# Splitting fetch from preparation of token tiles, and adding two directions' outputs from the PSUM bank

## The chip, the cores and the metric

The kernel runs on one core of a Trainium2 chip. The metric is device time of one execution in microseconds; three executions of the kernel before gave 3358.46, 3360.61 and 3367.17 us, so the median is 3360.61 us.

## The reference

One layer of a bidirectional encoder over 2048 tokens of width 1024, in float32. A layer norm gives `h`; one input projection feeds two head groups, and their outputs are concatenated into one output projection; then follow a layer norm, a squared-ReLU MLP and a last layer norm. The parts that matter here:

```python
def hybrid_mixer(h, w_in, ..., w_out):
    proj = h @ w_in
    ...
    y_ssd = ssd_bidir(z, xbc, dt_raw, conv_w, conv_b, dt_bias, a_log, d_skip, ssd_norm_g)
    y_rwkv = rwkv7_bidir(rw, mu_rwkv, w0, w_up, a0, a_up, g_up, k_k, k_a, r_k, lnx_g, lnx_b)
    y = jnp.concatenate([y_ssd, y_rwkv], -1).astype(h.dtype)
    return y @ w_out
...
# the end of ssd_bidir:   y = y * silu(z); y * rsqrt(mean(y*y) + RMS_EPS) * norm_g
# the end of rwkv7_bidir:
    _, ys = lax.scan(rwkv7_step, S0, inputs)
    y = ys[forward] + flip(ys[backward])
    y = ((y - mean) * lax.rsqrt(var + GN_EPS)) * lnx_g + lnx_b   # per head of 64
    return (y + bonus) * g
```

`rwkv7_step` is a recurrence over tokens, run once forward and once backward; the two outputs of a token are added before the group norm.

## The kernel before, in words

The kernel works in three phases. `phase_in` normalises, projects and runs most of the SSD group. `phase_rwkv` (line 936) runs the RWKV recurrence in chunks of 128 tokens, and weaves the output projection into it as filler for TensorE. `phase_mlp` (line 1358) follows.

**The recurrence.** There are 32 steps `u`. Step `u` treats head group `pg = u % 2` and chunk `s = u // 2`, both directions at once: the forward direction treats the tokens of chunk `s`, the backward direction those of chunk `15 - s` (`UN` is 16). Four generators make up the work of a step, and `weave` (line 1260) interleaves their pieces with fixed weights: `chain(u)` (line 1136), the serial part, has 12 pieces; `finish(u - 1)` (line 1207) gets weight 10 and runs from `FL` = 0.4 to `FH` = 1.0 of the chain; `merge`, `inverse` and `prep` prepare later steps.

`chain(u)` collects the outputs of both directions in one PSUM bank, `yp` (line 1154; the pool has one buffer), by the matmuls of lines 1165 and 1192. Line 1182 (`zt`), lines 1185 and 1186 carry the state to the next step of the head group on VectorE. At the end (lines 1194 to 1205) ScalarE copies each direction's outputs out of the bank (line 1202) and a DMA stores them to the scratch tensor `yaD` (line 1203). From `s` = 8 on, each token tile then has both directions' outputs in `yaD`. `finish` loads both (line 1213), adds them on GpSimd (line 1214), centres the sum per head with a matmul (line 1219), squares it on ScalarE (line 1222), sums the squares with a matmul (line 1225), takes the root and the reciprocal (lines 1228, 1230), scales, adds the bonus and multiplies by the gate (lines 1239 to 1249), and stores to `yR` (line 1250).

**The output projection.** `out_pieces` (line 785) is a generator of filler. It visits the 16 token tiles twice in one order: first with the SSD half of the weights, and a second time with the RWKV half, and then the layer norm. `load` (line 813) fetches a token tile from DRAM (residual `h`, outputs `yr`, in the first pass also the broadcast root mean squares `rsb`), scales `yr` on VectorE in the first pass (line 823), and splits it into a high and a low part on ScalarE (line 825) and GpSimd (line 827). `products` (line 830) does 24 matmuls (line 838) in eight pieces of three, and adds the results to `h` on VectorE (lines 841, 843). Most pools of this generator have two buffers a name. The next token is loaded ahead of the products of the present one (line 896).

**What sets the order.** `dense(ins, n)` (line 1074) is called at eight points of a step at most (once after each product of `chain` and of `merge` that has a weight). Each call adds a credit, and takes pieces from the filler until it has met a piece that yields `DENSE`; a piece that yields `HELD` ends the call and leaves at most one credit. `tc.issue_after` ties the filler's TensorE instructions behind the instruction given. In the second pass token `j` is held until step `FA + j` = 19 + `j`; tokens that do not fit are drained in `phase_mlp`, between its first preparations (lines 1434 to 1438). All loads and stores are issued by SyncE (SP), in one queue. The whole program is put in order by `tile.TileContext(nc, schedule_with_timeline_sim=True)` (line 1681): the written order is a priority among the instructions that are ready.

Of the kernel before, what the change touches and what calls it, by code (L numbers as in the profile page):

```python
# [9 lines left out]
F32 = mybir.dt.float32  # L10
F32R = mybir.dt.float32r
AF = mybir.ActivationFunctionType
ALU = mybir.AluOpType
# [3 lines left out]
P = 128  # L17
# [767 lines left out]
def out_pieces(k):  # L785
# [3 lines left out]
    with ExitStack() as ctx:  # L789
# [20 lines left out]
                yield  # L810
            k.wo = wh, wl

        def load(t, ys, first):
            h = wk.tile([P, D], F32, name="h")
            nc.sync.dma_start(h, k.hD[t])
            yr = wk.tile([P, 4, P], F32, name="yr")
            for g in range(2):
                nc.sync.dma_start(yr[:, 2 * g:2 * g + 2], ys[g][:, :, P * t:P * t + P].rearrange("a p t -> p a t"))
            if first:
                rsb = wk.tile([P, 2, P], F32, name="rsb")  # L820
                nc.sync.dma_start(rsb, rsD[:, t].unsqueeze(0).broadcast_to([P, 2, P]))
                for c in range(4):
                    nc.vector.scalar_tensor_tensor(yr[:, c], yr[:, c], ppc(k, "ng", c), rsb[:, c // 2], ALU.mult, ALU.mult)
            yh = wk.tile([P, 4, P], F32R, name="yh")
            nc.scalar.copy(yh, yr)
            yl = wk.tile([P, 4, P], F32R, name="yl")
            nc.gpsimd.tensor_tensor(yl, yr, yh, ALU.subtract)
            return t, h, yh, yl
# [62 lines left out]
        nc.sync.dma_start(rsD.rearrange("g c t -> (g c) t"), rt)  # L891
        yield
        order = [t for s in range(NT // 2, NT) for t in (NT - 1 - s, s)]
        ops = load(order[0], k.yS, True)
        for j in range(NT):
            nxt = load(order[j + 1], k.yS, True) if j + 1 < NT else None
            yield
            yield from products(ops, True)
            ops = nxt
        ws = weights(4)  # L900
        next(ws)
        for p in gates((0, 3)):
# [15 lines left out]
        for j in range(NT):  # L918
            while not ready(j):
                yield HELD  # L920
            if nxt:
                ops = nxt
            else:
                ops = load(order[j], k.yR, False)
                for _ in range(HL):
                    yield HELD
            while k.u < FA + j // FB:
                yield HELD
            nxt = load(order[j + 1], k.yR, False) if ready(j + 1) else None
            yield  # L930
            yield from products(ops, False, rows)
            k.finals = j + 1
            yield LAST


def phase_rwkv(k):
    nc, tc, I = k.nc, k.tc, k.I
    with ExitStack() as ctx:
# [32 lines left out]
        def pairs(ap):  # L971
            return ap.rearrange("a p t -> p a t")
# [163 lines left out]
        def chain(u):  # L1136
# [14 lines left out]
                return out, mm  # L1151


            yp = k.psy.tile([P, 2, 2, 2, 64], F32, name="yp")
            for c in range(2):
                yield
# [37 lines left out]
            ZV.pop(u)  # L1194
            fin = FIN[u] = []
            for d in range(2):
                nat = s if d == 0 else UN - 1 - s
                yv = yp[:, d].rearrange("p r c t -> p r (c t)")
                if d:
                    yv = yv[:, :, ::-1]  # L1200
                ya = sm.tile([P, 2, P], F32, name="ye")
                nc.scalar.copy(ya, yv)
                nc.sync.dma_start(pairs(k.yaD[pg][2 * d:2 * d + 2, :, P * nat:P * nat + P]), ya)
                if s >= UN // 2:
                    fin.append(nat)

        def finish(u):

            pg, fin = u % 2, FIN.pop(u)
            fin = [(nat, sm.tile([P, 2, P], F32, name="ya")) for nat in fin]  # L1210
            for nat, ya in fin:
                yo = sm.tile([P, 4, P], F32, name="yo")
                nc.sync.dma_start(yo, pairs(k.yaD[pg][:, :, P * nat:P * nat + P]))
                nc.gpsimd.tensor_tensor(ya, yo[:, 0:2], yo[:, 2:4], ALU.add)
            yield
            sds = []
            for nat, ya in fin:
                cp_ = k.ps.tile([P, 2, P], F32, name="ps")
                nc.tensor.matmul(cp_, rc[:, R_CEN:R_CEN + P], ya, start=True, stop=True)
                (nc.scalar.copy if CA else nc.vector.tensor_copy)(ya, cp_)  # L1220
                sq = wk.tile([P, 2, P], F32, name="sq")
                nc.scalar.activation(sq, cp_, AF.Square)
                yield
                vp = k.ps.tile([P, 2, P], F32, name="ps")
                nc.tensor.matmul(vp, k.cst[:, C_BLK:C_BLK + P], sq, start=True, stop=True)
                yield
                sd = sm.tile([P, 2, P], F32, name="sd")
                nc.scalar.activation(sd, vp, AF.Sqrt, bias=k.eps[:, 2:3], scale=1.0 / 64)
                for pr in range(2):
                    nc.vector.reciprocal(sd[:, pr], sd[:, pr])  # L1230
                sds.append(sd)
            for (nat, ya), sd in zip(fin, sds):
                tok = slice(P * nat, P * nat + P)
                bon = wk.tile([P, 2, P], F32, name="bon2")
                nc.sync.dma_start(bon, pairs(k.bD[pg][:, :, tok]))
                gate = wk.tile([P, 2, P], F32, name="gate")
                nc.sync.dma_start(gate, pairs(k.gD[pg][:, :, tok]))
                yield
                nc.vector.tensor_tensor(ya, ya, sd, ALU.mult)
                for pr in range(2):  # L1240
                    p = 2 * pg + pr
                    if TA:
                        nc.scalar.activation(ya[:, pr], ya[:, pr], AF.Identity, scale=ppc(k, "lnx_g", p), bias=ppc(k, "lnx_b", p))
                    else:
                        nc.vector.tensor_scalar(ya[:, pr], ya[:, pr], ppc(k, "lnx_g", p), ppc(k, "lnx_b", p), ALU.mult, ALU.add)
                yield
                nc.gpsimd.tensor_tensor(bon, ya, bon, ALU.add)
                o = wk.tile([P, 2, P], F32, name="o")
                (nc.gpsimd if OG else nc.vector).tensor_tensor(o, bon, gate, ALU.mult)
                nc.sync.dma_start(pairs(k.yR[pg][:, :, tok]), o)  # L1250
                k.final[nat] += 1
# [29 lines left out]
        for u in range(-AH, U):  # L1281
            jobs = []
            if 0 <= u - 1 and FIN[u - 1]:
                fin = finish(u - 1)
                if FE:
                    next(fin)
                jobs.append((fin, 10, FL, FH, 0))
            if 0 <= u + MG < U:
                jobs.append((merge(u + MG), 5, ML, 0.9, PM))
            if 0 <= u + AH - 1 < U:  # L1290
                jobs.append((inverse(u + AH - 1), 16, IL, IH, PI))
            if u + AH < U:
                jobs.append((prep(u + AH), 18, 0.0, PH, PP_))
            k.u = u
            jobs.append((k.ssd, SR, 0.0, 1.0, PS))
            weave(chain(u) if u >= 0 else iter([None] * 12), jobs)
# [388 lines left out]
```

## Time and profile before

| | us |
|---|---|
| median of three executions | 3360.61 |
| lowest, highest | 3358.46, 3367.17 |
| the profiled execution | 3365.71 |
| its span from the first to the last instruction | 3363.9 |
| TensorE busy in that span | 2999.4 |
| VectorE busy | 2166.7 |
| ScalarE busy | 1535.1 |
| GpSimd busy | 1584.2 |

All times in the profile come from that one execution and count from its first instruction. PE is TensorE's matmul, PEld its weight load, DVE is VectorE, ACT is ScalarE, POOL is GpSimd, SPq is the queue of SyncE that issues the DMAs; L1202 is line 1202 of the kernel. A group row reads: line, engine, operation, output<-inputs, shapes, count | busy us, mean ns of one | idle us of the engine just before them and what ended it. A row of waits reads: who waited for whom: us in total, times, longest. A row of the timeline reads: start, duration in us, engine, line, operation, tiles, count, and in brackets the idle time before it.

### The profile page before, as it was taken

The numbers are of one execution on the slowest core, as the hardware profiler recorded it, in microseconds if no ns is written. First come the engines' busy times: TensorE is split into PE (matmuls) and PEld (weight loads), VectorE is DVE, ScalarE is ACT, GpSimd is POOL, SyncE is SP. The second block draws the span as 40 slices with busy tenths as digits, with TensorE's granted clock in tenths as the row PEclk, the third lists the DMA queues.
The fourth block names the chain that finished last, engine by engine and source line by source line (L and its number), as shares of the span: only waits on it lengthen the run. The fifth ranks groups of instructions, "written<-read, shape, count | busy, mean of one in ns | idle before, by whom it ended". The sixth has DMA issues, their size and how long they took to land. (4 is left out here: it accounts for less than half of the span.)

```text
span 3363.9 us, 63959 instructions
## 1 busy us (share of the span) xinstructions
PE 2999.4 (89%) x23783; PEld 2394.6 (71%) x23783; DVE 2166.7 (64%) x3671; ACT 1535.1 (46%) x2993; POOL 1584.2 (47%) x1972
## 2 busy tenths in 40 slices
PE   5979999988887799898898886999899989999997
PEld 3767877766675577676666664888787868887886
DVE  7798556667666455554577658767877744466446
ACT  3556323333334445455565544544544553344333
POOL 0352124444445333334466665555566335555645
PEclk9989999889886688897798887999999989999998
DMA  6445355776778666666666554777799475566554
GB/s 209 135 157 185 120 148 176 199 214 195 201 205 251 150 165 161 155 167 163 170 181 174 142 155 152 234 252 234 258 323 314 141 297 190 198 213 212 189 197 153
DMA packets 728183, 650.23 MB, mean 193 GB/s; under 512 B 204064, under 2 KB 578496, under 8 KB 727232
## 3 DMA queue, kind: packets, MB, share of 16 engines
q1 hardware_dynamic: 727872, 646.15, 62.5%
q8 instruction: 187, 3.06, 0.4%
q14 instruction: 124, 1.02, 0.1%
HBM read 403.43 MB, written 242.57 MB: 192 GB/s over the span
## 5 line engine op out<-in xcount | busy, mean ns | idle before, releaser
L1553 DVE TENSOR_TENSOR ul<-ul,uh 128x1024 fp32r<-128x1024 f32 x112 | 241.3, 2156 | 293.9 <-ACT uh L1552 293.6
L1553 POOL TENSOR_TENSOR pl<-pl,ph 128x1024 fp32r<-128x1024 f32 x112 | 287.9, 2575 | 277.9 <-ACT ph L1552 277.8
L1507 PE MATMUL ps<-hh,wh 128*128 128x512 f32 x896 | 352.2, 394 | 19.8 <-ACT wh L1370 6.6
L266 PE MATMUL psg<-hh,wh 128*128 128x512 f32 x864 | 357.2, 414 | 7.3 <-ACT u L285 6.6
L1611 PE MATMUL ps<-ph,uh 128*128 128x512 f32 x896 | 349.0, 392 | 10.4 <-ACT ph L1552 8.7
L1611 PE MATMUL ps<-pl,uh 128*128 128x512 f32 x896 | 351.6, 393 | 5.0 <-POOL pl L1553 5.0
L267 PE MATMUL psg<-hh,wl 128*128 128x512 f32 x864 | 354.5, 410 | 0.0
L268 PE MATMUL psg<-hl,wh 128*128 128x512 f32 x864 | 353.2, 410 | 1.4 <-DVE hl L236 1.4
L1507 PE MATMUL ps<-hl,wh 128*128 128x512 f32 x896 | 350.6, 392 | 1.5 <-DVE hl L1430 1.4
L1507 PE MATMUL ps<-hh,wl 128*128 128x512 f32 x896 | 351.0, 392 | 0.9 <-DVE wl L1371 0.9
L1611 PE MATMUL ps<-ph,ul 128*128 128x512 f32 x896 | 350.4, 392 | 0.0
L1371 DVE TENSOR_TENSOR wl<-wa,wh 128x512 fp32r<-128x512 f32 x217 | 209.5, 970 | 88.9 <-ACT wh L1370 87.9
L1065 POOL TENSOR_TENSOR ltmp<-ln,la 128x30 f32<-128x30 f32 (+10 forms) x480 | 123.6, 258 | 255.7 <-DMA la<-ad 225.6
L1552 ACT CAST ph<-pl 128x1024 fp32r<-128x1024 f32 x112 | 117.7, 1051 | 274.2 <-DMA pl<-pD 274.2
L1370 ACT CAST wh<-wa 128x512 fp32r<-128x512 f32 x217 | 133.0, 618 | 207.2 <-POOL wa L1343 100.2
L1507 PEld LDWEIGHTS ps<-hh,wh 128*128 128x128 f32 x896 | 169.8, 190 | 59.2 <-ACT wh L1370 7.9
L266 PEld LDWEIGHTS psg<-hh,wh 128*128 128x128 f32 x864 | 169.6, 196 | 47.4 <-ACT u L285 8.1
L1611 PEld LDWEIGHTS ps<-ph,uh 128*128 128x128 f32 x896 | 169.4, 189 | 47.0 <-ACT ph L1552 9.5
L1611 PEld LDWEIGHTS ps<-pl,uh 128*128 128x128 f32 x896 | 169.8, 190 | 43.9 <-POOL pl L1553 8.7
L268 PEld LDWEIGHTS psg<-hl,wh 128*128 128x128 f32 x864 | 168.4, 195 | 39.7 <-issue 3.4
L1507 PEld LDWEIGHTS ps<-hl,wh 128*128 128x128 f32 x896 | 169.5, 189 | 37.5 <-DVE hl L1430 1.8
L267 PEld LDWEIGHTS psg<-hh,wl 128*128 128x128 f32 x864 | 169.7, 196 | 36.3 <-issue 2.6
(322 smaller groups left out, 7087.6 us busy)
## 6 DMA issues: line engine op xcount, KB each, us to landing
uD<-ua SPq DMA_DIRECT2D x224, 256.0 KB, 2.9
ul<-uD SPq DMA_DIRECT2D x112, 512.0 KB, 4.6
pl<-pD SPq DMA_DIRECT2D x112, 512.0 KB, 3.7
wa<-in_w_fc_dram SPq DMA_DIRECT2D x124, 256.0 KB, 3.4
pD<-sc SPq DMA_DIRECT2D x112, 256.0 KB, 4.2
rk<-rk SPq DMA_DIRECT2D x64, 384.0 KB, 4.7
h<-hD SPq DMA_DIRECT2D x48, 512.0 KB, 4.0
eD<-et SPq DMA_DIRECT2D x32, 514.0 KB, 2.7
```

The source lines that it names most:

```text
L266: nc.tensor.matmul(pt, wh[:, c], hh[:, c], start=(c == 0), stop=False)
L267: nc.tensor.matmul(pt, wl[:, c], hh[:, c], start=False, stop=False)
L268: k.lag = nc.tensor.matmul(pt, wh[:, c], hl[:, c], start=False, stop=(c == KC - 1))
L1065: eng.tensor_tensor(tv, ln[:, 0:m, r:r + 1].broadcast_to([P, m, w]), la[:, r:r + 1, r + 1:16].broadcast_to([P, m, w]), ALU.mult)
L1370: nc.scalar.copy(hi, x)
L1371: nc.vector.tensor_tensor(lo, x, hi, ALU.subtract)
L1507: nc.tensor.matmul(pt, x, y, start=(n == 0 and i not in (2, 3)), stop=(n == 11 and i not in (1, 5)), skip_group_check=True)
L1552: nc.scalar.copy(hi, x)
L1553: eng.tensor_tensor(lo, x, hi, ALU.subtract)
L1611: nc.tensor.matmul(banks[j], x, z, start=(g == 0 and s == 0), stop=(g == NG - 1 and s == 5))
```

## The change

`load` becomes two functions. `fetch` issues the DMAs only; `prepare` has the VectorE scaling and the split. A helper `after` runs the products of a token and calls `prepare` for the next token when the sixth of the eight pieces comes up. The first token of the first pass is prepared four held calls behind its fetch, and a fifth held call follows; in the second pass a token that is not prefetched is prepared behind its two held calls.

In `chain`, from `s` = 8 on, the other direction's stored outputs are loaded at the start of the step into `yo`, and at its end a VectorE add takes the bank and `yo` and writes the sum to `ya`, which `finish` uses at once. The store of these steps, and `finish`'s load and GpSimd add, are gone. In `finish` a second `yield` stands between the square and its matmul, and its weight is 12 in place of 10.

```diff
-        def load(t, ys, first):
+        def fetch(t, ys, first):
             h = wk.tile([P, D], F32, name="h")
             nc.sync.dma_start(h, k.hD[t])
...
                 nc.sync.dma_start(rsb, rsD[:, t].unsqueeze(0).broadcast_to([P, 2, P]))
+                return t, h, yr, rsb
+            return t, h, yr, None
+
+        def prepare(raw):
+
+            t, h, yr, rsb = raw
+            if rsb is not None:
                 for c in range(4):
                     nc.vector.scalar_tensor_tensor(yr[:, c], yr[:, c], ppc(k, "ng", c), rsb[:, c // 2], ALU.mult, ALU.mult)
             yh = wk.tile([P, 4, P], F32R, name="yh")
...
-        ops = load(order[0], k.yS, True)
+        def after(pieces, raw, n=5):
+
+            ops = None
+            for i, p in enumerate(pieces):
+                if p is DENSE:
+                    if i == n and raw:
+                        ops = prepare(raw)
+                    yield p
+            return ops
+
+        raw = fetch(order[0], k.yS, True)
+        for _ in range(4):
+            yield HELD
+        ops = prepare(raw)
+        yield HELD
         for j in range(NT):
-            nxt = load(order[j + 1], k.yS, True) if j + 1 < NT else None
+            raw = fetch(order[j + 1], k.yS, True) if j + 1 < NT else None
             yield
-            yield from products(ops, True)
-            ops = nxt
+            ops = yield from after(products(ops, True), raw)
...
-                ops = load(order[j], k.yR, False)
+                raw = fetch(order[j], k.yR, False)
                 for _ in range(HL):
                     yield HELD
+                ops = prepare(raw)
...
-            nxt = load(order[j + 1], k.yR, False) if ready(j + 1) else None
+            raw = fetch(order[j + 1], k.yR, False) if ready(j + 1) else None
             yield
-            yield from products(ops, False, rows)
+            nxt = yield from after(products(ops, False, rows), raw)
...
+            nats = [s, UN - 1 - s]
+            others = []
+            for d in range(2) if s >= UN // 2 else ():
+                yo = sm.tile([P, 2, P], F32, name="yo")
+                nc.sync.dma_start(yo, pairs(k.yaD[pg][2 - 2 * d:4 - 2 * d, :, P * nats[d]:P * nats[d] + P]))
+                others.append(yo)
+
             yp = k.psy.tile([P, 2, 2, 2, 64], F32, name="yp")
...
-                ya = sm.tile([P, 2, P], F32, name="ye")
+                ya = sm.tile([P, 2, P], F32, name="ye", bufs=4)
+                if s >= UN // 2:
+                    nc.vector.tensor_tensor(ya, yv, others[d], ALU.add)
+                    fin.append((nat, ya))
+                    continue
                 nc.scalar.copy(ya, yv)
                 nc.sync.dma_start(pairs(k.yaD[pg][2 * d:2 * d + 2, :, P * nat:P * nat + P]), ya)
-                if s >= UN // 2:
-                    fin.append(nat)
...
-            fin = [(nat, sm.tile([P, 2, P], F32, name="ya")) for nat in fin]
-            for nat, ya in fin:
-                yo = sm.tile([P, 4, P], F32, name="yo")
-                nc.sync.dma_start(yo, pairs(k.yaD[pg][:, :, P * nat:P * nat + P]))
-                nc.gpsimd.tensor_tensor(ya, yo[:, 0:2], yo[:, 2:4], ALU.add)
             yield
...
                 nc.scalar.activation(sq, cp_, AF.Square)
+                yield
                 yield
...
-                jobs.append((fin, 10, FL, FH, 0))
+                jobs.append((fin, 12, FL, FH, 0))
```

More of the change, by code (lines that the diff above doesn't have):

```diff
@@ L1196, in chain @@
             for d in range(2):
-                nat = s if d == 0 else UN - 1 - s
+                nat = nats[d]
                 yv = yp[:, d].rearrange("p r c t -> p r (c t)")
```

## The prediction

> **What bounds the kernel now.** I read the profile from coarse to fine: the page, the stages, then who waits for whom in the stages that the change touches.
>
> ```profile
> span 3363.9 us, 63959 instructions
> ```
>
> ```profile
> 1150.00:1565.00 415.00, 376.30 (x6753) 291.85 (x6751) 231.25 (x566) 199.13 (x571) 141.35 (x489) 0.87 0.60 155
> 1565.00:1640.00 75.00, 65.97 (x1169) 51.95 (x1163) 43.42 (x96) 47.29 (x130) 42.16 (x103) 0.81 0.82 221
> 1640.00:1978.00 338.00, 298.38 (x5020) 225.60 (x5020) 225.96 (x449) 191.66 (x523) 204.40 (x451) 0.88 0.60 157
> 1978.00:2072.00 94.00, 51.47 (x211) 38.51 (x210) 68.01 (x92) 43.19 (x79) 62.69 (x51) 0.71 0.51 164
> 2072.00:3364.00 1292.00, 1240.04 (x5424) 1018.80 (x5422) 813.73 (x782) 584.04 (x807) 697.53 (x358) 0.98 0.66 225
> ```
>
> The second answer gives, for each stretch, its length, the busy time (and instructions) of PE, PE's weight loads, VectorE (DVE), ScalarE (ACT) and GpSimd (POOL), then PE's granted clock, the DMA share and GB/s. TensorE is the busiest engine of every long stage, but the change lies only in the recurrence, from 1150 on: the first pass of the output projection (1150 to 1565), the turn between the passes (to 1640), the second pass with `finish` (to 1978), and the passage to the MLP (to 2072). There PE idles 11 to 12%, in the passage 45%, and its granted clock is 0.71 to 0.88 against 0.98 in the MLP. So time can be had from PE's waits and from the slow clock behind them. Who ends those waits:
>
> ```profile
> PE ch L1150 <- DVE zt L1182: 23.2, 11, 4.0
> PE psg L838 <- ACT yh L825: 14.6, 1, 14.6
> ```
>
> ```profile
> PE ps L1219 <- POOL ya L1214: 9.8, 5, 6.1
> PE ch L1150 <- DVE zv L1169: 9.4, 5, 3.8
> PE ps L1225 <- ACT sq L1222: 9.1, 6, 4.0
> ```
>
> ```profile
> PE ps L1219 <- POOL ya L1214: 9.5, 1, 9.5
> ```
>
> The first pair is 1150 to 1565 (us, times, longest), the second 1565 to 1980, the single row the passage. `finish` thus costs PE 9.8 + 9.1 = 18.9 us in the second pass and 9.5 us once in the passage. The first pass loses 23.2 us to a late `zt`, and 14.6 us once at its start.
>
> **Part two of the change first: outputs added from the bank.** This is one chain end as it is now, then the last one:
>
> ```profile
> 1752.24 0.66 ACT L1202 COPY ye<-yp 128x256 f32<-128x256 f32 x2
> 1752.27 1.40 DVE L1186 TENSOR_TENSOR zz<-zt,dtab 128x256 f32<-128x256 f32 x1
> ...
> 1753.60 0.74 DVE L1026 TENSOR_TENSOR ra<-ps,rc 128x256 f32<-128x256 f32 x2
> 1754.27 1.21 DVE L1007 TENSOR_TENSOR bk<-bk,E 128x256 f32<-128x256 f32 x2
> ...
> 1755.52 0.68 PE L1165 MATMUL yp<-kr,zv 64*64 64x64 f32 x16
> ```
>
> ```profile
> 1978.09 0.65 ACT L1202 COPY ye<-yp 128x256 f32<-128x256 f32 x2
> 1978.37 1.75 DVE L1230 RECIPROCAL sd<-sd 128x128 f32<-128x128 f32 x2
> ...
> 1987.53 1.22 PE L1219 MATMUL ps<-ya,rc 128*128 128x256 f32 x2 [9.48 <-POOL ya L1214]
> ```
>
> Prices of one instruction, and what the DMA queue waited for at the store (1565 to 1990):
>
> ```profile
> L1202 ACT COPY ye<-yp 128x256 f32<-128x256 f32 x64 | 20.7, 377 | 11.2 <-ACT nm L1134 9.6 <-PE yp L1192 1.2
> L1214 POOL TENSOR_TENSOR ya<-yo 128x256 f32<-128x256 f32 x32 | 24.0, 751 | 21.9 <-DMA yo<-yaD 21.5
> L740 DVE TENSOR_TENSOR t<-t,ps 128x256 f32<-128x256 f32 x60 | 24.5, 413 | 3.0 <-PE ps L724 2.9
> ```
>
> ```profile
> SPq L1203 <- ACT ye L1202: 15.8, 7, 4.2
> ```
>
> Removed, in each of the 16 chains of the second half: two ACT copies (0.377 us each), two stores, two loads behind them, two POOL adds (0.751 us each): 12.1 us of ACT and 24.0 us of POOL, neither the bound. Added: two VectorE adds per chain with one operand in PSUM. That form at this size is L740, 0.413 us, so 32 x 0.413 = 13.2 us on an engine busy 226 of 338 us; most of it lies in idle time.
>
> What is on a path is the round trip. At the end of the recurrence the bank is read at 1978.09 and L1219 starts at 1987.53: 9.4 us. An add straight from the bank starts when VectorE is free: at 1978.4, or behind the two reciprocals at 1980.1. Two adds take 0.83 us, so L1219 can start at 1979.3 to 1981.0, 6.5 to 8.2 us earlier; I take 7.5. The passage behind it should move whole, because the MLP's first loads sit right behind the last store of `finish`:
>
> ```profile
> 2001.20 0.36 SPq L1250 DMA_DIRECT2D yR<-o  x1
> 2001.66 0.90 SPq L1388 DMA_DIRECT2D h<-hD  x2
> ```
>
> In the second pass the 9.8 us on L1214 should go, and the 9.1 us on L1225 too, through the extra `yield` between the square and its matmul. PE then meets the next late thing, `zv` on VectorE (9.4 us above), so I count three quarters of 18.9: 14 us, with bounds of 0 and 18.9. The clock adds a little:
>
> ```profile
> 1206.00:1225.00 19.00, 18.07 (x212) 14.17 (x213) 9.87 (x26) 5.89 (x18) 4.78 (x19) 0.50 0.53 124
> ...
> 1735.00:1741.00 6.00, 5.53 (x27) 4.12 (x28) 2.52 (x4) 3.90 (x12) 1.67 (x8) 0.50 0.74 165
> 1851.00:1857.00 6.00, 5.22 (x37) 3.97 (x38) 3.06 (x4) 3.56 (x11) 5.49 (x6) 0.50 0.64 107
> ```
>
> Two stretches of 6 us at half clock stand in the second pass right behind waits on L1225. At most half of 12 us is lost there; I take 3 (bounds 0 and 6).
>
> The new wait. `yp` has one bank, and the next chain's L1165 cannot write it until it has been read. ACT frees it at 1752.90 now. VectorE at that moment is working off the end of its own chain: an add right behind L1186 ends at 1753.67 + 0.83 = 1754.5, ahead of L1165 at 1755.52, and costs nothing. An add placed behind L1026 and L1007 ends at 1755.48 + 0.83 = 1756.3, 0.8 us late, or 13 us over 16 chains. The chain's end is written ahead of those, so I take 4 us (bounds 0 and 13). Behind the add on VectorE stand L1026 and L1007, for which TensorE's next Gram products and transposes wait: this is in the same 4 us.
>
> The new loads of `yo` are issued at the start of a chain, a whole chain ahead of use, and read rows that were stored at least one chain before that, so their landing is hidden. In the queue the wait above (15.8 us of SP standing still ahead of the stores) vanishes, and the loads no longer wait for those stores to land. In their place the new load waits for the adds of the previous chain, since two buffers serve both directions; I put this at no gain. `bufs=4` and the weight of 12 for `finish` I cost at nothing: the copies are held one step longer, and the steps of `finish` stay behind 0.4 of a chain, as now.
>
> **Part one: fetch and prepare apart.** What it aims at is VectorE standing still for a tile that has not landed:
>
> ```profile
> L823 DVE SCALAR_TENSOR_TENSOR yr<-yr,pp,rsb 128x128 f32<-128x128 f32 x64 | 19.8, 366 | 68.4 <-DMA yr<-yS 38.7 <-DMA rsb<-rsD 13.3 <-POOL ln L1066 9.3
> ```
>
> That is 68.4 us of idle VectorE ahead of 64 instructions, and the late `zt` is its echo. But is it the written place that puts L823 there? The program is laid out with `schedule_with_timeline_sim=True`, and the trace shows how far that moves things:
>
> ```profile
> 1129.17 0.46 SPq L1237 DMA_DIRECT2D gate<-gD  x1
> ...
> 1181.08 1.16 DVE L823 SCALAR_TENSOR_TENSOR yr<-yr,pp,rsb 128x128 f32<-128x128 f32 x4 [3.36 <-POOL ltmp L1065]
> ...
> 1227.23 0.50 PE L838 MATMUL psg<-woh,yh 128*128 128x512 f32 x1
> ```
>
> L1237 belongs to `finish`, which first runs in step 17, behind the whole first pass, and yet it is issued at 1129. The L823 at 1181.08 is the fifth token's, and its code stands ahead of the fourth token's products, which start at 1227.23: it ran 46 us early, as soon as a buffer was free and the tile was reckoned to be there. Writing it five of a token's eight pieces later (16 of the 415 / 16 = 26 us that a token takes) leaves buffer and landing as they are. So I expect L823 in the same place, waiting as now, and count nothing. The five held calls at the start push four pieces back; at three matmuls of up to 0.50 us (the last row above) that is some 6 us of PE work, which finds room in the turn, where the first token of the second pass waits for its step 19 anyway. If that cover is gone it costs the 6 us. The products also begin elsewhere within a chain; this can move waits either way.
>
> **The sum.** -14 - 3 + 4 - 7.5 + 0 = -20.5 us, made against the profiled execution's 3365.7 us. That run is 5.1 us above the median of 3360.6; the difference is carried over: 3340 us.
>
> By the Trainium skill, "TensorE: Matmul & The Clock Gate", Part 1, the clock halves only after an idle window of about 3.4 us. The trace does not bear the threshold out in the first pass: the 23.2 us on `zt` came in waits of 2.1 us on average and 4.0 at most, and the 19 us at 0.50 lie among them. If the page held, the clock term of rival 1 below would all but vanish, and that rival would end 23 us higher.
>
> **Rivals.**
> 1. *Part one does what it says too.* For it: 68.4 us of waits that a later place would avoid. Against: the 46 us above. It adds three quarters of the 23.2 us on `zt` (17 us), part of the 14.6 us at the start (5, about half of what the 6 us leave), and clock: from 0.87 to 0.98 over 415 us would be 46 us, of which I take half (23), since the chain's small matmuls gain less. 3340 - 45 = 3295 us.
> 2. *Waits only change owner.* In the second pass PE works 298 of 338 us whatever ends its waits, and VectorE's chain (L1169, 9.4 us) takes over. Only the passage is won: 3360.6 - 7.5 = 3353 us, within 0.3%. The Trainium skill, "Perfetto Trace Analysis", Identifying the Most-Contended Engine, points here: it says to relieve the busiest engine first, and this change relieves ACT and POOL and loads VectorE.
> 3. *VectorE holds the bank* (slower). If the adds come behind L1026 and L1007, the bank is freed at 1756.3 instead of 1752.9, 3.4 us later. Where L1165 stands right behind the eviction all of it is a wait: 16 x 3.4 = 54 us against a gain of 24.5 without the 4 us: 3390 us. It is slower by 0.3% from 2.2 us per chain on. Against: at the chain end above only 0.8 us would show.
>
> **Numbers.** 0.3%, about 10 us, is what a measurement of this kernel can tell from no change. Forecast 0.50, with a range of its own of 3327 (18.9, 6 and 8.2 won, nothing added) to 3356 (7 of the 14, the bank at 13). Rivals 0.16, 0.18, 0.16. Faster: 0.46 of the forecast's 0.50 (the rest falls above 3350) and rival 1, 0.62; same: 0.04 + 0.18 = 0.22; slower: 0.16. The range reaches down to rival 1, and up to 3372, where rival 3 begins.
>
> **What would show it.** Right: L1219 has no wait on a far engine, and starts within 3 us of the last L1192; the stage of 338 us shrinks by 10 to 15; L823 still waits for `yS` some 40 us in all. Wrong: L823's waits fall under 15 us and the first pass shrinks by 30 or more (rival 1); waits of L1165 on VectorE of 2 us and more at chain ends (rival 3); the first L1507 no earlier against the last L1192 than now.

## The result, and the profile after

The change made the kernel slower: 3384.18 us median of 4 runs (3382.43 to 3394.67), against 3361.27 of the kernel before in the same session. The ratio is 1.0084, with a 95% interval of 1.0058 to 1.0110. My forecast was 3340 us, faster. The profiled execution took 3382.43 us:

```profile
span 3380.6 us, 63807 instructions
```

To see where the time went I cut both traces at instructions that both have: the `zt` at the end of steps 0, 16, 19 and 29 (line 1182 before, L1210 after), the end of the last `yp` matmul, and the first up matmul of the MLP.

| stretch | before | after | difference |
|---|---|---|---|
| start to `zt` of step 0 | 1149.9 | 1145.5 | -4.4 |
| step 0 to 16: first pass | 419.5 | 441.0 | +21.5 |
| step 16 to 19: turn | 91.8 | 101.1 | +9.3 |
| step 19 to 29: second pass | 283.8 | 283.8 | 0 |
| step 29 to the last `yp` | 33.0 | 32.5 | -0.5 |
| last `yp` to first up matmul: passage | 83.6 | 77.9 | -5.7 |
| MLP | 1302.3 | 1298.8 | -3.5 |

The stretches of after, in the columns of the prediction (length, then the busy time of PE, weight loads, DVE, ACT and POOL, then PE's granted clock):

```profile
1145.50:1586.50 441.00, 373.03 (x6827) 286.68 (x6829) 230.62 (x569) 201.56 (x579) 143.48 (x503) 0.87 0.60 148
1586.50:1687.60 101.10, 84.19 (x1303) 66.03 (x1298) 53.54 (x118) 52.83 (x145) 45.48 (x123) 0.71 0.60 158
1687.60:1971.40 283.80, 239.32 (x4253) 183.24 (x4251) 198.61 (x416) 158.65 (x433) 159.28 (x369) 0.91 0.56 144
```

In the first pass every engine has nearly the same number of instructions to do as before, and PE idles 441.0 - 373.0 = 68 us, against 419.5 - 380.8 = 38.7 us in the kernel before. So the loss is waiting, and it sits in the half of the change that I had counted at nothing. Who waits there (us, times, longest):

```profile
DVE yr L830 <- DMA yr<-yS: 90.3, 15, 8.5
ACT at L1046 <- DVE kr L1045: 81.9, 15, 8.0
...
PE ps L1054 <- ACT bkt L1056: 54.6, 13, 5.7
ACT vrev L1061 <- DMA rk<-rk: 45.2, 15, 10.0
```

Part one was to shorten VectorE's wait for the tile (L823 is now L830). It rose from 38.7 to 90.3 us, once in every step, and a chain hangs on it: ScalarE's L1046 waits for VectorE, PE's L1054 for ScalarE. PE's waits on `zt`, 23.2 us before, are nearly gone (0.7 us); 54.6 us on `bkt` stand in their place. The one long wait at the start of the pass, 14.6 us on `yh` before, is there still, now on `bkt` and just ahead of the stretch counted here. One step in order of time:

```profile
1259.46 1.27 POOL L834 TENSOR_TENSOR yl<-yr,yh 128x512 fp32r<-128x512 f32 x1
...
1260.76 0.88 SPq L818 DMA_DIRECT2D yr<-yS  x2
...
1263.04 1.14 DVE L830 SCALAR_TENSOR_TENSOR yr<-yr,pp,rsb 128x128 f32<-128x128 f32 x4 [7.82 <-DMA yr<-yS]
...
1264.21 0.88 DVE L1045 TENSOR_TENSOR kr<-ps,rc 64x256 f32<-64x256 f32 x2
...
1264.67 0.36 ACT L1046 COPY at<-ps 64x256 f32<-64x256 f32 x1 [7.32 <-DVE kr L1045]
1264.94 0.36 ACT L1056 COPY bkt<-ps 128x256 f32<-128x256 f32 x1
...
1265.36 0.68 PE L1054 MATMUL ps<-cst,bk 64*128 64x64 f32 x4 [5.00 <-ACT bkt L1056]
```

Read it from the top, with the lines between left out. GpSimd subtracts `yl` behind the inverse's last rounds, which frees the `yr` buffer. The transfer queue then fetches the next tile. VectorE has stood at the scaling for 7.82 us, and L1045, which needs nothing from the tile, stands behind it in VectorE's queue. So ScalarE and then TensorE wait for a tile whose products run over 70 us later.

What moved is the place in the chain. Measured from one `zt` to the next, a token's products began at 0.54 to 0.70 of a chain before (from the fifth token on), and begin at 0.02 to 0.03 now: 1252.2 between the `zt` of 1251.4 and 1279.3, say. The scaling stood at 0.91 to 0.97, behind nearly all of the preparation of keys, and now stands at 0.33 to 0.42, in the middle of it.

Part two looks like its forecast at the end of the recurrence:

```profile
2003.22 0.69 PE L1220 MATMUL yp<-ra,zv 128*64 128x64 f32 x16
2004.01 0.76 DVE L1231 TENSOR_TENSOR ye<-yp,yo 128x256 f32<-128x256 f32 x2
...
2004.49 0.70 PE L1244 MATMUL ps<-ye,rc 128*128 128x256 f32 x2 [0.58 <-DVE ye L1231]
```

The matmul that waited 9.48 us for GpSimd's sum starts 0.6 us after the last `yp` ends (2003.91). In the turn and the second pass (1586 to 1971) PE waits for other things instead:

```profile
PE ps L1054 <- ACT bkt L1056: 17.3, 4, 10.4
PE ch L1171 <- ACT rs L1187: 9.0, 2, 8.3
PE ch L1171 <- DVE zv L1197: 8.4, 4, 6.3
PE ch L1171 <- DVE zt L1210: 7.4, 4, 5.5
...
PE ps L1251 <- ACT sq L1247: 5.1, 2, 4.2
...
PE yp L1193 <- DVE ye L1231: 0.6, 1, 0.6
```

### The profile page after: what moved, and what is told of

Its sections match the earlier page's. It is cut to its first block, busy times and chain, and to the rows that moved or that the text cites. A ratio compares the mean times of both kernels' runs of the same rounds, so it can differ in the third digit from the quotient of the medians.

```text
span 3380.6 us, 63807 instructions
## 1 busy us (share of the span) xinstructions
PE 2976.0 (88%) x23783; PEld 2379.4 (70%) x23783; DVE 2187.9 (65%) x3703; ACT 1524.9 (45%) x2961; POOL 1563.2 (46%) x1940
## 5 line engine op out<-in xcount | busy, mean ns | idle before, releaser
L1637 PEld LDWEIGHTS ps<-pl,uh 128*128 128x128 f32 x896 | 169.7, 189 | 45.2 <-POOL pl L1579 10.2
L1637 PEld LDWEIGHTS ps<-ph,uh 128*128 128x128 f32 x896 | 169.2, 189 | 45.8 <-ACT ph L1578 10.6
L1533 PEld LDWEIGHTS ps<-hh,wl 128*128 128x128 f32 x896 | 169.3, 189 | 38.0 <-DVE wl L1397 3.0
```

Source lines behind the costliest of these rows:

```text
L1533: nc.tensor.matmul(pt, x, y, start=(n == 0 and i not in (2, 3)), stop=(n == 11 and i not in (1, 5)), skip_group_check=True)
L1637: nc.tensor.matmul(banks[j], x, z, start=(g == 0 and s == 0), stop=(g == NG - 1 and s == 5))
```

## The experiments

Theory A: the five held calls shift the tokens (a token is one tile of 128 tokens in the filler's work) within the chain, and this costs the time. Rivals: B, the later written preparation costs it; C, part two does. All ratios are to the kernel before on the same chip, with 95% intervals.

### The two parts, and the two halves of part one

**Part one alone.** 

> The kernel before with part one alone: fetch and prepare apart, prepare five pieces into the token ahead of it, and the five held calls at the start of the first pass. Theory A: the 21.5 us that the first pass has lost (zt of step 0 to zt of step 16: 419.5 before, 441.0 after) come from the held calls, which shift the tokens from the end of a chain to its start. Theory B: they come from the later written preparation itself. Both expect here a first pass of 437 to 445 us and a time of 3380 to 3393 (the upper end if the turn's 9 us belong to part one too). Theory C: part two costs them (VectorE's adds, the new loads); then the first pass stays at 417 to 423 and the time at 3358 to 3366.

**Part two alone.** 

> The kernel before with part two alone: adds from the bank, loads of the other direction at the start of a chain, the additional step and the weight of 12 for the output steps; fetch and preparation in one as before. Theories A and B: first pass 417 to 423 us; the passage from the last yp matmul to the first up matmul 77 to 79 us as in the whole change (before 83.6); second pass proper (zt of step 19 to 29) 270 to 284, the lower end if my 14 us were there and only part one ate them; time 3340 to 3358. Theory C: 3375 to 3390 with the first pass at 437 or more.

**The held calls alone**, on the kernel before:

```diff
         ops = load(order[0], k.yS, True)
+        for _ in range(5):
+            yield HELD
```

> The kernel before with nothing but five held calls between the first tile's load and the first token of the first pass; loads and preparation stay in one. Theory A: first pass 435 to 445 us, waits of VectorE on yS about 80 to 100 us instead of 38.7, time 3375 to 3390. Theory B: first pass 417 to 425, waits on yS about 40, time 3358 to 3368.

**The whole change without the held calls:**

```diff
-        raw = fetch(order[0], k.yS, True)
-        for _ in range(4):
-            yield HELD
-        ops = prepare(raw)
-        yield HELD
+        ops = prepare(fetch(order[0], k.yS, True))
```

> The whole change but without the five held calls: the first tile is fetched and prepared at once, all later ones five pieces behind their fetch. Theory A: first pass 417 to 425 us, time 3350 to 3365. Theory B: first pass 435 to 445, time 3375 to 3388. My prediction's reading that the written place of the preparation changes nothing (it is put where its buffer and tile are reckoned to be there) expects VectorE's waits on yS at about 40 us here, as in the kernel before; if the split alone removes them, they fall under 15.

| | load in one | fetch and prepare apart |
|---|---|---|
| before's outputs, no held calls | 1 | not run |
| before's outputs, five held calls | 1.0149 (1.0121 to 1.0177) | 1.0152 (1.0123 to 1.0181) |
| part two, no held calls | 0.9957 (0.9934 to 0.9981) | 0.9959 (0.9938 to 0.9980) |
| part two, five held calls | not run | 1.0084 (1.0058 to 1.0110) |

The columns agree in both rows that were run in both: the split does nothing. Five held calls cost 1.5% (3403.06 against 3357.56, 45 us), and 1.25% on top of part two. Part two alone gains 0.4% (3342.46, 15 us). B and C fall. Both kernels with held calls and without part two took longer than I had expected under A: 3407.87 us for part one alone against at most 3393, and 3403.06 for the held calls alone against at most 3390. The held calls alone carry the signature of the whole change, at the lines of that kernel (over this slightly wider stretch, which takes in the long wait at the start, the last row is 69.3 us in the whole change):

```profile
DVE yr L823 <- DMA yr<-yS: 89.5, 15, 8.2
ACT at L1027 <- DVE kr L1026: 80.8, 15, 7.7
...
PE ps L1035 <- ACT bkt L1037: 70.6, 14, 17.1
```

The split without held calls leaves VectorE's idle time ahead of the scaling at 70.4 us in all, as before (68.4):

```profile
L830 DVE SCALAR_TENSOR_TENSOR yr<-yr,pp,rsb 128x128 f32<-128x128 f32 x64 | 19.7, 366 | 70.4 <-POOL ln L1083 25.8 <-DMA yr<-yS 20.5 <-DMA rsb<-rsD 15.3
```

### The number of held calls, or the place

The whole change with ten held calls, and with eight (`range(7)`):

```diff
-        for _ in range(4):
+        for _ in range(9):
             yield HELD
         ops = prepare(raw)
         yield HELD
```

> The whole change with ten held calls in front of the first pass instead of five. In the program's order the tokens then begin at 0.51 of a chain (0.97 with five, 0.66 with none), and the scaling of a tile stands at 0.86 of a chain on VectorE (0.22 with five, 0.89 with none). Theory A (the place in the chain decides, above all where VectorE waits for the tile): first pass 402 to 412 us as without held calls, time 3335 to 3352, although twice as many calls are held. Theory D (held calls cost by their number, some 9 us each): first pass 470 or more, time above 3400.

> The whole change with eight held calls: tokens begin at 0.23 of a chain, the scaling stands at 0.69 of a chain on VectorE. Theory A: VectorE no longer waits in front of the preparation of keys (waits of ScalarE L1046 on VectorE under 30 us instead of 82), first pass 402 to 425, time 3335 to 3365. Theory D: above 3400. If it is TensorE's own order that costs (a token's first matmuls at the start of a chain, theory A2), 0.23 is still early, and the time stays at 3365 to 3385.

Ten: 3349.30 us, 0.9975 (0.9953 to 0.9997). Eight: 3342.25 us, 0.9964 (0.9950 to 0.9978). Against 0.9959 without held calls, eight cost 2 us and ten 5, both less than the intervals can tell from nothing, while five cost 42: theory D, a price per call, falls. Eight calls speak against A2 as well, which expected 3365 to 3385. The waits on yS are 26.4 us with ten and 45.8 with eight, those of L1046 on VectorE 23.9 and 14.4. The first pass with ten took 421.0 us, more than the 412 I allowed, but not for its waits: TensorE idled only 27.1 us in it, and was busy 393.9 us at a granted clock of 0.82.

### Is it VectorE's standing still?

Theory A now has two forms: A1, the loss is VectorE's wait at the scaling; A2, the loss is TensorE's own order, with a token's matmuls at the start of a chain. The four scalings are put in the queue behind the last VectorE instruction of the chain before (an edge of order, no wait):

```diff
+                with tc.issue_after(k.anchor.ins) if k.anchor else ExitStack():
                     for c in range(4):
                         nc.vector.scalar_tensor_tensor(yr[:, c], ...)
...
-                        nc.vector.tensor_tensor(zn, zt, dn...)
+                        k.anchor = nc.vector.tensor_tensor(zn, zt, dn...)
```

> The whole change, five held calls included; only the four scalings of a tile on VectorE are put in the queue behind the last VectorE instruction of the chain before (order alone, no wait). TensorE's tokens still begin at 0.97 of a chain; the scaling stands at 0.11 of a chain, one and a half chains later than before, so that its tile has long landed. Theory A1 (VectorE standing still at L830 in front of the preparation of keys is the loss): waits on yS under 15 us instead of 90, first pass 402 to 412, time 3335 to 3350, nearly all of the loss given back. Theory A2 (TensorE's order is the loss): the waits on yS vanish too, but the first pass stays at 430 to 445 and the time at 3375 to 3390.

> The split and part two without held calls, and the scalings put behind the last VectorE instruction of the chain before: tokens begin at 0.67 of a chain, the scaling stands at 0.11. Theory A1: waits on yS under 10 us instead of 20 to 39, TensorE's waits on zt under 8 us instead of 22, first pass 385 to 400, time 3318 to 3335: this would be what part one aimed at. Rival: the late zt has another cause than the scaling in front of it; then zt keeps 15 us or more and the time stays at 3335 to 3347.

With five held calls 3382.10 us, 1.0079 (1.0057 to 1.0101): no gain. Without: 3350.52, 0.9979 (0.9961 to 0.9996), not better than unpinned and outside both ranges, though TensorE's waits on `zt` are gone. The waits on yS did vanish in both, and A1 alone falls with them. A2 had the time with held calls right, but not the first pass: it took 466.2 us, longer than either form allowed, even without the long wait at the start, 16.0 us, which here falls behind the `zt` of step 0 and in the kernels without pinned scalings ahead of it. What TensorE waits for there is a load:

```profile
ACT vrev L1062 <- DMA rk<-rk: 116.7, 14, 10.3
...
DVE kr L1031 <- DMA rk<-rk: 61.9, 14, 6.8
...
PE ch L1172 <- ACT rs L1188: 61.4, 14, 6.4
```

`rk` comes later than in the whole change (116.7 us at ScalarE instead of 45.2). The DMA queue's own timeline shows why:

```profile
1301.53 0.33 SPq L856 DMA_DIRECT2D hD<-h  x1
1311.99 1.22 SPq L1091 DMA_DIRECT2D nd<-ln  x2
...
1314.98 2.92 SPq L1094 DMA_DIRECT2D ni<-nd  x2
1317.95 0.62 SPq L1019 DMA_DIRECT2D rk<-rk  x1
```

The queue issues nothing from 1301.86 to 1311.99: it stands at the store of the inverse's result until GpSimd has finished it, and the load of `rk` stands behind. Over the first pass this adds up:

```profile
SPq L1091 <- POOL ln L1088: 129.2, 15, 10.3
```

So I formed theory G: no engine's place is bad in itself; a queue worked off in order stands at something that is late, and passes its wait to whatever is behind. First it was VectorE at the scaling, then the transfer queue at that store.

### The store, and the tile's load, taken out of that queue

The store issued by GpSimd itself, behind its own last round:

```diff
-                nc.sync.dma_start(nd[:, :, q], ln[64 * q:64 * q + 64])
+                nc.gpsimd.dma_start(nd[:, :, q], ln[64 * q:64 * q + 64])
```

**With five held calls and the pinned scalings:**

> Five held calls and the scalings pinned behind the chain before, as in the pinned run at 3382 us, where the waits on yS had vanished but the transfer queue stood 129 us at the inverse's store (behind GpSimd) and the loads of rk behind it came 62 us (VectorE) and 117 us (ScalarE) late. Here that store alone is issued by GpSimd itself. Theory G (no engine's place in itself, but whichever queue stands in order behind something late: first VectorE at L830, then the transfer queue at the store): waits on rk under 60 us together instead of 179, first pass 402 to 425 us, time 3335 to 3358. Theory A2 (a token's matmuls at the start of a chain are the loss on TensorE itself): 3370 to 3390 whatever the queues wait for.

3337.53 us, 0.9938 (0.9922 to 0.9954): 45 us faster than with the store in the old queue, although the tokens still begin at the start of the chain (0.99 to 0.05, from the second token on). A2 falls, and G has the time right:

```profile
ACT vrev L1062 <- DMA rk<-rk: 78.3, 15, 8.8
...
PE ch L1172 <- ACT rs L1188: 22.2, 11, 4.9
...
DVE kr L1031 <- DMA rk<-rk: 21.9, 11, 5.2
```

The waits on `rk` are 100 us together, not under 60 as I expected, but they stand where TensorE waits 22 us for them, not 61.

**The store moved, five held calls, scalings not pinned:**

> The whole change with five held calls, the inverse's store issued by GpSimd, the scalings not pinned. Theory G says that both waits have to go: the scaling still stands at 0.22 of a chain and waits for its tile, whose buffer comes free behind GpSimd's inverse: waits on yS 70 us or more, L1046 on VectorE 60 or more, first pass 430 to 442, time 3370 to 3388. If the store alone was what the pinned run gained by: first pass 405 to 422, time 3335 to 3350.

3377.72 us, 1.0062 (1.0041 to 1.0083). As G expects, the time falls little by either edit alone (3382 and 3378, from 3384 for the whole change), and by 47 us with both. The waits are those that G expects, too:

```profile
DVE yr L830 <- DMA yr<-yS: 80.7, 19, 9.1
ACT at L1046 <- DVE kr L1045: 78.6, 16, 8.6
...
PE ps L1054 <- ACT bkt L1056: 63.7, 14, 12.9
```

But its first pass is shorter than G allowed (424.3 us for 430 to 442). How long TensorE idles in the first pass separates the waits from the clock:

| kernel | first pass | TensorE idle in it | of this the long wait at the start | granted clock |
|---|---|---|---|---|
| before, two profiles | 419.5, 417.5 | 38.7, 40.6 | lies ahead | 0.87, 0.88 |
| whole change | 441.0 | 68.0 | lies ahead | 0.87 |
| pinned | 466.2 | 89.5 | 16.0 | 0.85 |
| store moved | 424.3 | 56.7 | lies ahead | 0.88 |
| pinned and store moved, two profiles | 417.3, 409.2 | 52.8, 50.0 | 11.8, 10.0 | 0.90, 0.91 |

Without the wait at the start, the whole change idles 68 us, the pinned kernel 73, the one with the store moved 57, and the one with both 41 and 40, about as much as the kernel before. So the two edits together take away the idle time that the held calls had brought, and neither does so alone. The rest of the 47 us is not idle time of the first pass; in part it is TensorE's busy time there (364.5 and 359.2 us instead of 373.0, at a higher granted clock), and the remainder was not followed.

**The tile's loads issued by GpSimd**, five held calls:

```diff
-                nc.sync.dma_start(yr[:, 2 * g:2 * g + 2], ...)
+                (nc.gpsimd if first else nc.sync).dma_start(yr[:, 2 * g:2 * g + 2], ...)
```

> The whole change with five held calls; in the first pass the two loads of a token's yr tile are issued by GpSimd, behind its own subtraction yl, which frees the buffer, instead of by the transfer queue that stood 95 us for it. If VectorE's wait at L830 in front of the preparation of keys is the loss (A1), it stays (yS 70 us or more, L1046 on VectorE 65 or more) and the time stays at 3370 to 3390. If the transfer queue's standing still and the late loads of rk behind it are the loss, the waits of vrev on rk fall from 45 to under 20 us and the time to 3335 to 3358.

3368.71 us, 1.0036 (1.0017 to 1.0056): between the two expectations, a little below A1's range. The waits of `vrev` on `rk` fell to 14.1 us, those on yS stayed (87.6). Of the 42 us some 16 came back (1.0084 to 1.0036): the late `rk` behind the transfer queue's standing still seems the smaller part of the loss, VectorE's wait the larger.

**Without held calls**, the store moved, and both edits:

> Split and part two without held calls, the inverse's store issued by GpSimd: the transfer queue's 34.5 us at that store vanish. Theory G, if that queue matters in this phase too: 3320 to 3335. If in this phase nothing urgent stands behind it: 3336 to 3346, like the run without held calls.

> No held calls, scalings pinned behind the chain before and the store issued by GpSimd: the candidate for a version faster than both kernels. Theory G: waits on yS under 10 us, on rk under 60 together (109 in the pinned run without held calls), waits of TensorE on zt under 10; first pass 395 to 410, time 3320 to 3338. If a third late thing takes their place: 3338 to 3352.

Two misses: 3355.76 us, 0.9995 (0.9972 to 1.0018), and 3365.44 us, 1.0023 (1.0008 to 1.0038). The second is slower than the kernel without these edits, 0.9959 (0.9938 to 0.9980); the first seems so, but the intervals just overlap. With both, the waits on yS and on `zt` are gone, and a third late thing took their place in the transfer queue, again in nearly every step:

```profile
SPq L815 <- DMA hD<-h: 74.5, 14, 6.5
SPq L1090 <- DMA nd<-ln: 68.5, 14, 7.8
```

Edits that give 47 us at one place of the tokens lose some 20 at another. What exactly the two stalls hold up there was not followed further.

### What brings part two's gain

The kernel before, unchanged: 

> The kernel before unchanged, for a second profile of it: 3345 to 3370 us. It tells how far one profiled execution's stages can be trusted: first pass 405 to 420 us, turn 90 to 94, second pass 276 to 286, passage 83 to 85.

Two buffers for the first half's copies:

```diff
-                ya = sm.tile([P, 2, P], F32, name="ye", bufs=4)
+                ya = sm.tile([P, 2, P], F32, name="ye", bufs=4) if s >= UN // 2 else sm.tile([P, 2, P], F32, name="yf")
```

> Part two alone, but with the first half's copies of outputs in two buffers of their own as in the kernel before; the four buffers serve the second half only. In the first pass the engines' orders are the same with part two and without it, so if the shorter first pass of part two alone (404.5 us against 419.5 and 417.5 in two profiles of the kernel before) comes from the four buffers, it is 415 to 421 here and the time 3350 to 3358. If it was the variation from run to run, the first pass can be anything from 403 to 420 and the time is that of part two, 3337 to 3348.

The old steps of `finish`:

```diff
                 nc.scalar.activation(sq, cp_, AF.Square)
                 yield
-                yield
...
-                jobs.append((fin, 12, FL, FH, 0))
+                jobs.append((fin, 10, FL, FH, 0))
```

> Part two alone without the additional step between the square and its matmul and with the weight of 10 as before. My prediction put 9.1 of the 18.9 us of the second pass to that step. If so: TensorE's waits on the square (L1222's successor) 8 us or more, second pass 279 to 286 us instead of 273.5, time 3346 to 3356. If the adds from the bank alone bring it: second pass 271 to 278, time 3337 to 3347.

Part two alone, unchanged: 

> Part two alone, unchanged, for a second profile on another chip: 3337 to 3350 us. If its short first pass (404.5 us) was the variation from run to run, it can come out anywhere between 403 and 420 here; if it belongs to part two it is 402 to 407 again.

The kernel before again took 3350.85 us, in one execution. The others: 3347.14 us, 0.9974 (0.9960 to 0.9988), with two buffers; 3349.29, 0.9973 (0.9955 to 0.9992), with the old steps; 3343.28, 0.9975 (0.9956 to 0.9993), part two again. These intervals overlap, so here are the stretches:

| kernel | first pass | turn | second pass | passage |
|---|---|---|---|---|
| before, two profiles | 419.5, 417.5 | 91.8, 87.2 | 283.8, 285.5 | 83.6, 83.4 |
| held calls alone | 439.9 | 95.6 | 297.6 | 92.6 |
| part two, two profiles | 404.5, 413.7 | 93.0, 98.2 | 273.5, 272.8 | 77.4, 77.4 |
| with two buffers in the first half | 419.0 | 93.7 | 277.4 | 78.8 |
| with the old steps of `finish` | 420.0 | 94.7 | 285.7 | 76.3 |
| split and part two, no held calls | 403.9 | 92.0 | 276.2 | 77.3 |

The passage shrinks by 6 us either way. The turn grows by some 5 us, which is what two profiles of one kernel differ by. The first pass is no gain of part two: it took 404, 414 and 420 us in kernels whose instructions on TensorE, VectorE and ScalarE stand in one order there, with four buffers and with two.

The second pass is shorter by about 10 us: 275.0 on average over the four profiles with the additional step, against 284.7 in the kernel before. In the one profile without that step it took 285.7, but this doesn't show that the step decides it. Here is the second pass of the kernel before, of part two and of part two with the old steps:

```profile
1661.20:1945.00 283.80, 251.98 (x4267) 191.18 (x4263) 197.79 (x396) 162.84 (x450) 171.52 (x386) 0.88 0.62 162
```

```profile
1643.20:1916.70 273.50, 241.85 (x4264) 185.49 (x4261) 195.78 (x415) 159.47 (x432) 158.38 (x369) 0.91 0.58 151
```

```profile
1657.50:1943.20 285.70, 256.86 (x4221) 195.68 (x4221) 195.84 (x416) 158.46 (x430) 160.34 (x371) 0.85 0.56 145
```

TensorE idles 31.8, 31.7 and 28.8 us: with the old steps it waits no longer. What differs is its busy time, 252, 242 and 257 us, and with it the granted clock, 0.88, 0.91 and 0.85. Over all profiles, idle time falls from 33.2 to 31.1 us on average and busy time from 251.5 to 243.9. So some 2 of the 10 us are waits, and the rest is work done at a higher clock. Whether part two or its step raises the clock, or the executions differ by chance as in the first pass, stays open; the timed runs give the kernel with the old steps the same ratio as part two.

**A version faster than both** is the one with five held calls, pinned scalings and the moved store. It ran again beside part two alone:

> Five held calls, scalings pinned, the store issued by GpSimd, unchanged, beside part two alone on the same chip: 3332 to 3345 us; against part two alone 0 to 8 us faster. Waits on yS under 15 us and on rk 80 to 110 together, as in its first profile.

3338.79 us, 0.9955 (0.9938 to 0.9971), as the first time faster than both kernels. That it is faster than part two alone (3343.28, 0.9975) is not shown, as the intervals overlap. Its waits on `rk` were 89.7 us together.

## Why the prediction was wrong

**The step that failed** is the sentence at the end of part one: "The products also begin elsewhere within a chain; this can move waits either way", counted at nothing. I had priced the held calls by the work that they push back, at most 6 us and covered by the turn. The runs show 45 us, from the place and not from the work: eight and ten calls push back more and cost little. The profile of before had the warning. It showed how close VectorE's queue runs to its tile (38.7 us of waits at L823), and an instruction that waits at an engine's queue can only be priced with what stands behind it. The scaling waited at 0.91 to 0.97 of a chain, behind nearly all of the preparation of keys; at 0.33 to 0.42 it waits in front of much of it. That this wait costs the time is shown by the pair of edits alone: taken away by itself, it gave its place to the next one.

**Right:** the written place of `prepare` decides nothing that can be measured. With and without the split the time agrees twice (1.0152 and 1.0149, 0.9959 and 0.9957), the scaling stands at 0.94 to 0.96 of a chain with the split (0.91 to 0.97 before), and VectorE's idle time ahead of it is 70.4 us against 68.4. "L823 still waits for `yS` some 40 us in all" is wrong for the whole change, where it is 90.3 us, and with the split alone only 20.5 of the 70.4 us are put down to yS.

**The 14 us of the second pass** measured about 10 in part two alone, and 0 in the whole change. The mechanism was wrong in the main. The waits on GpSimd's sum did go, 8.5 and 6.5 us in the two profiles of before (turn and second pass together), but other waits took their place, and idle time fell by 2 us. PE's waits on the square were 9.1 and 12.9 us before, 7.3 and 7.2 in part two, and 7.7 with the old steps, so the extra `yield` isn't shown to do what I priced it at:

```profile
PE ps L1230 <- ACT sq L1226: 7.2, 3, 4.9
```

In the whole change TensorE idles 44.5 us in the second pass, 13 to 16 more than in part two alone: there the held calls' new waits took the gain. **The passage** came to 5.7 us against 7.5: L1244 came 8.9 us earlier against the last `yp` (0.6 for 9.5), more than I took, but from it to the first up matmul it was 77.3 us (2004.49 to 2081.8) instead of 74.1 (1987.53 to 2061.6). **The 3 us of the clock** were too few if the higher clock in the second pass of part two is its doing; that can't be told from the clock's own variation (below). **The new wait on the bank**, 4 us with a bound of 13, is 0.6 us: the adds come in time behind the chain's end, and rival 3 is out. The DMA queue's wait of 15.8 us at the stores became one of 7.5 us (4 times) at the new load, for the adds. Not forecast is the turn, some 5 us longer with part two. And PE's idle share in the first pass was 9% (38.7 of 415 us), not 11 to 12% as I read it; only the turn and the second pass idle that much.

**Rival 2**, waits only changing owner, describes TensorE's idle time in the second pass of part two best, though part two gained 9 to 15 us in the timed runs and not 7.5. In the second pass of the whole change the length stayed at 283.8 us for another reason: PE's busy time fell from 251.98 to 239.32 us at a higher clock, and its idle time grew as much. By the Trainium skill, "Perfetto Trace Analysis", Identifying the Most-Contended Engine, the busiest engine is to be optimized first. Here that could not mean less work for TensorE: it was busy 373 of 441 us in the first pass, but the time lost came from queues that stood still, and the two edits that won it back were one store on another queue and one edge of order.

**Rival 1** named what part one aims at, 45 us faster. Pinned, the scaling did lose its waits for the tile, and TensorE those on `zt`, but without held calls the gain was eaten by late `rk` loads (TensorE waited 44.7 us on `rs`).

**Open:** why the held calls also add idle time to the second pass, though the tokens there begin by their own conditions: TensorE idles 46.5 us there with the held calls alone and with part one alone, 44.5 in the whole change, against 31.9 and 34.6 in the kernel before. And why they lengthen the passage by 9 us (92.6) without part two, but not with it (77.9).

## What to carry to other kernels

A filler's phase against the main loop is a parameter of its own: before shifting it, list for each in-order queue (engines and the DMA queue) what waits there for something late, and what will stand behind that wait at the new place. A wait removed from one queue can reappear in the next queue that stands at the same late producer, here GpSimd's inverse, so edits have to be tried together: two that were worth next to nothing singly gave 47 us as a pair, and the same pair lost time at another phase. In a program laid out by a scheduler, moving a line need not move the instruction: here the scaling stayed where its buffer and its tile had put it. And when a stretch gets shorter, ask whether its idle time fell or only its busy time.

## What was unexpected of the hardware

The same instructions, in the same order on TensorE, VectorE and ScalarE, took 403.9 to 420.0 us in the first pass, in the seven profiles of kernels without held calls and without the edits to the queues. The granted clock goes with it. In part two alone, the two profiles differ by 9 us both in the length and in TensorE's busy time:

```profile
1145.70:1550.20 404.50, 372.33 (x6832) 288.68 (x6831) 231.07 (x570) 202.37 (x579) 142.26 (x494) 0.90 0.63 163
```

```profile
1135.90:1549.60 413.70, 381.31 (x6833) 295.89 (x6831) 230.88 (x571) 202.27 (x579) 138.49 (x486) 0.87 0.61 159
```

At 0.90 instead of 0.87 of the full clock, 6832 matmuls take 372 us instead of 381. A short wait is enough to go with a slow stretch: the 19 us at half clock that the prediction shows (1206 to 1225) begin at a wait of 2.57 us on `zt`, which ends at 1206.93. The stretch ahead of step 0 varied from 1135.9 to 1149.9 us between those seven profiles, and the MLP from 1298.5 to 1313.1 over all. TensorE's idle time in the first pass varied less, from 32.2 to 40.6 us. So the length of a stretch in one profile is good to some 16 us here; differences under that need a second profile, the timed runs, or the idle time beside the busy time.
